# Two-layer encoder trunk: MLP passes that share their PSUM banks, and the making of the first product's forms divided anew over the engines

## The chip, the cores and the metric

The kernel runs on one core of one Trainium2 chip. A core has a matrix engine (TensorE, PE in the profile, with its weight loads as PEld), a vector engine (VectorE, DVE), a scalar engine (ScalarE, ACT), a general engine (GpSimd, POOL) and a queue of its own for transfers (SyncE, SP). Each engine works off its own list of instructions in order and waits for the others by semaphores. Products land in PSUM, which is used here as 8 banks of 128 x 512 float32; everything else lies in SBUF. The metric is the device time of one execution in microseconds (us).

## The reference

The input is 256 tokens of 2048 values. Layer 0 mixes tokens with a Conformer convolution, layer 1 with latent attention; each is followed by the MLP that this document is about. Cut to that:

```python
def sq_relu_mlp(h, w1, w2):
    return jnp.square(jax.nn.relu(h @ w1)) @ w2

for layer in range(2):                       # D_MODEL = 2048, D_FF = 8192
    x = x + mixer(rms_norm(x, norm_mixer_g[layer]))
    h = rms_norm(x, norm_mlp_g[layer])
    x = x + sq_relu_mlp(h, mlp_w1[layer], mlp_w2[layer])
```

All of it is float32, and the products are made with near float32 accuracy: each operand is split into a rounded part `hi` and a rest `lo`, and hi x hi, hi x lo and lo x hi are added (three matmuls for one product).

## The kernel before

**Chunks and the stream.** Both products of the MLP are cut into *units*, each with one transfer of 1 MB of weights (`raw`), and units into *chunks*. The chunks of a whole layer stand in one list, `chunks`, and `stream` (L423) writes the program from it. `prep` of a chunk splits its weights: ACT writes `hi` (L420), DVE writes `lo` (L421). `run` of a chunk emits its matmuls. Before the `run` of chunk n, the preparations up to chunk n + 5 are written (`WB` = 6 buffers), or up to n + 4 where the chunk is marked `tight` (`LOOK_UP` = 5). Since each engine works in order, this order is all there is of scheduling. Small jobs stand in a list `todo`; one of them is popped before each preparation (L457).

**First product (`up_units`, L485).** The 8192 columns of `w1` are cut into 4 parts `q`, each into 8 pairs `p` of two units. An up unit has two chunks of 8 x (one matmul of 512 columns and one of 256) into one PSUM bank. After its second chunk ACT copies the bank to `U` (L510). When both units of a pair are done, three jobs enter `todo`: `square` (DVE: sum of the two halves, L522, and max(0, v) x v in one instruction, L525 or L536), an empty one, and `part`, which splits the result into `hi` and `lo` by ACT and DVE. For pairs in `SEVENS`, `square` also makes seven forms of the result in a tile `W` by three subtractions on POOL (L529, L532, L533); their split parts are `sh` and `sl`. For the other pairs the parts are `gh` and `gl`. The pairs of a part are made in the order `MADE`.

**Second product (`down_units`, L547).** A *pass* is one part `q` times one half `n2` of the 2048 output columns: 8 passes per layer. 5 of its 8 pairs (3 or 2 in the last part) are multiplied by a scheme of 7 products in place of 8 (a *seven unit*, four chunks: `one`, `two`, `t13`, `t24`, for whose weights DVE makes sums in a tile `T`, L672 and L685); the other pairs are *plain units* of two chunks. The seven sums live in seven banks (P1, P2, P4, Q3, Q5, Q6, Q7); the plain products add into P2, Q3, P4 and an eighth, Q0. So while seven banks are held, one is left for an up unit. After the last seven unit `early` evicts P1, Q5, Q6, Q7 (two ACT copies, L587 and L588; four DVE additions; four DVE updates of the residual `xs`, L564). After the last plain unit `end` adds the other four banks to `xs` (L564).

**The order of chunks.** The up units of part 0 come first. Then, for each part, its two passes, `n2` = 0 and 1, are woven with the 16 up units of the next part, eight per pass: `MIX` = (2, 1, 1, 2, 1, 1, 2) says how many halves of seven units follow each up unit; three plain units close the pass, with the eighth up unit after the first of them. The last part's passes run alone.

Of the kernel before, what the change touches and what calls it, by code (L numbers as in the profile page):

```python
# [14 lines left out]
AF = mybir.ActivationFunctionType  # L15
# [67 lines left out]
def trunk_kernel(  # L83
# [339 lines left out]
    def stream(chunks, todo, pool):  # L423
# [49 lines left out]
    def mlp(layer, ssq, next_gain, finish=None, before=None, last_w1=None):  # L473
# [11 lines left out]
        def up_units(hs, q, p, extra):  # L485
# [4 lines left out]
            def up_unit(b):  # L490
                ps = []

                def chunk(h):
# [20 lines left out]
                    return Chunk(prep, run, [square, lambda: None, part] + extra if b == 1 else [], now=out)  # L514
# [4 lines left out]

            def square():  # L520
                v = held["u"][:, :, :S]
                nc.vector.tensor_tensor(v, v, held["u"][:, :, S:], op=ALU.add)  # L522
                if p in sevens:
                    f = f_tile()
                    nc.vector.scalar_tensor_tensor(  # L525
                        out=f[:, 0:4, :].rearrange("p (b t) n -> p b (t n)", b=2), in0=v, scalar=0.0, in1=v,
                        op0=ALU.max, op1=ALU.mult,
                    )
                    nc.gpsimd.tensor_tensor(  # L529
                        f[:, 4:6, :], f[:, 0:1, :].broadcast_to([P, 2, P]), f[:, 1:3, :], op=ALU.subtract  # L530
                    )
                    nc.gpsimd.tensor_tensor(f[:, 6, :], f[:, 1, :], f[:, 5, :], op=ALU.subtract)  # L532
                    nc.gpsimd.tensor_tensor(f[:, 7, :], f[:, 3, :], f[:, 6, :], op=ALU.subtract)  # L533
# [13 lines left out]
        def down_units(mp, hs, q, n2):  # L547
# [9 lines left out]
            banks, seen = {}, set()  # L557
# [16 lines left out]
            def plain(p, k, part, n, t):  # L574
                gh, gl = (a[:, k, t * P : (t + 1) * P] for a in hs[p])
                bs = n - na
                mm(outs[t, n], gh, gl, part[0][:, bs, :], part[1][:, bs, :], p == last_plain and k == 1)

            def early():
# [24 lines left out]
                return [first, second, third, fourth]  # L604

            def end():
                for t, n in ((0, nb), (1, nb), (1, na), (0, na)):
# [47 lines left out]
            def seven_unit(p):  # L655
# [4 lines left out]
                def run(names):  # L660
                    def fn(parts):
                        for name, f, key, i in names:
                            part = parts[key]
                            mm(name, *gh_gl(f), part[0][:, i, :], part[1][:, i, :],
                               p == last_seven and name in ("P1", "Q5", "Q6", "Q7"))
# [21 lines left out]
                def t24(raw, parts):  # L687
# [9 lines left out]
                        now=todo_early if p == last_seven else None,  # L697
# [3 lines left out]
            def todo_early():  # L701
                first, *others = early()
                first()
# [10 lines left out]
        with ExitStack() as cx:  # L714
# [17 lines left out]
            hs = {}  # L732
            for unit in ups(hs, 0):
                put(unit)
            for q in range(PARTS):
                now, hs = hs, {}
                more = ups(hs, q + 1) if q < PARTS - 1 else []
                for n2 in range(NNB // 2):
                    units = down_units(mp, now, q, n2)
                    if not more:  # L740
                        for unit in units:
                            put(unit)
                        continue
                    halves = [(units[p], cs) for p in SEVENS[layer][q] for cs in ((0, 1), (2, 3))]
                    for n in MIX:
                        put(more.pop(0))
                        chunks[-1][0].chunks[1].tight = n == 1
                        for unit, cs in halves[:n]:
                            put(unit, cs)
                        del halves[:n]  # L750
# [993 lines left out]
```

## Time and profile before

| | |
|---|---|
| median of 3 runs | 1973.39 us (1971.7 to 1975.42) |
| the profiled execution | 1973.36 us, of which the profile's span is 1971.2 us |
| granted TensorE clock, mean | 0.998 |
| MLP of layer 0 | about 318.6 to 970 us of the span |
| MLP of layer 1 | about 1271.9 us to the end |
| six passes woven with up units, layer 0 | 84.9, 87.4, 84.8, 87.5, 87.1, 84.5 us |

The six passes are the stretches from 409.8, 494.7, 582.1, 666.9, 754.4 and 841.5 us to 926 us; each boundary is the start of a pass's first up unit. In the profile a row gives line, engine, operation, `out<-in` tiles and shapes. Busy time of PE is not a measure of its work alone, since matmuls overlap and their ends are modelled: the distance between the starts of two matmuls says more. A time in square brackets is idle time of the engine ahead of the instruction, with what ended it.

### The profile page before, as it was taken

How to read it: one execution, taken by the hardware profiler on the slowest of the kernel's cores; microseconds unless marked ns; L12 is line 12 of the kernel's file. 1: busy time of each engine (PE TensorE's matmuls, PEld its weight loads, DVE VectorE, ACT ScalarE, POOL GpSimd, SP SyncE). 2: the span in 40 equal slices, each digit the busy share in tenths (PEclk: the TensorE clock that was granted, in tenths of full speed). 3: DMA queues.
4: the chain of work that ended last, by engine and by line, in shares of the span. 5: the costliest groups of instructions: out<-in, count | busy, mean ns of one | idle time of the engine just before them, and what ended most of it. 6: DMA issues, size and time to landing. Idle time of an engine off the chain costs nothing.

```text
span 1971.2 us, 28450 instructions
## 1 busy us (share of the span) xinstructions
PE 1937.5 (98%) x10850; PEld 1685.6 (86%) x10850; DVE 1623.1 (82%) x2241; ACT 1108.2 (56%) x1555; POOL 348.9 (18%) x289
## 2 busy tenths in 40 slices
PE   7999999999999999999999999999999999999998
PEld 7999888888888888888899998888888888888886
DVE  5999866688898898989976675567989898888987
ACT  5556655565555564555566665555645555565544
POOL 5999300210110111000001410002011002010000
PEclk9999999999999999999999999999999999999999
DMA  8666457657566666756646445665766666657663
GB/s 238 177 189 176 147 185 192 194 169 225 152 212 193 194 198 185 217 170 211 213 143 183 121 143 188 196 185 161 214 187 208 182 209 191 192 179 207 224 203 107
DMA packets 407112, 367.62 MB, mean 186 GB/s; under 512 B 15416, under 2 KB 351936, under 8 KB 406720
## 3 DMA queue, kind: packets, MB, share of 16 engines
q1 hardware_dynamic: 405952, 363.63, 61.7%
q10 hardware_dynamic: 1024, 2.17, 0.3%
q8 instruction: 85, 1.39, 0.3%
q14 instruction: 51, 0.42, 0.1%
HBM read 363.68 MB, written 2.10 MB: 186 GB/s over the span
## 4 chain that ended last, share of the span: by engine, by line
PE 85%; DVE 6%; POOL 3%; ACT 3%; issue 2%; DMA 0%; SPq 0%; POOLq 0%; DVEq 0%; ACTq 0%
PE acc L504 20%; PE acc L197 14%; PE acc L195 14%; PE acc L196 14%; PE acc L505 10%; DVE lo L421 3%; PE acc L816 3%; PE acc L815 3%; PE acc L814 3%; POOL W L529 1%; DVE T L685 1%; ACT hi L420 1%; ACT sh L420 1%; POOL W L533 1%; POOL W L532 1%
## 5 line engine op out<-in xcount | busy, mean ns | idle before, releaser
L504 PE MATMUL acc<-xt,hi 128*128 128x512 f32 x2048 | 717.4, 393 | 0.0
L421 DVE TENSOR_TENSOR lo<-raw,hi 128x1024 fp32r<-128x1024 f32 (+1 forms) x512 | 582.8, 1162 | 46.7 <-ACT hi L420 46.0
L420 ACT ACTIVATE hi<-raw 128x1024 fp32r<-128x1024 f32 (+1 forms) x512 | 495.0, 994 | 143.3 <-PE acc L196 86.6
L505 PE MATMUL acc<-xt,lo 128*128 128x256 f32 x2048 | 574.1, 280 | 0.0
L504 PEld LDWEIGHTS acc<-xt,hi 128*128 128x128 f32 x2048 | 384.4, 188 | 87.5
L505 PEld LDWEIGHTS acc<-xt,lo 128*128 128x128 f32 x2048 | 385.2, 188 | 3.7
L197 PE MATMUL acc<-lo,sh 128*128 128x512 f32 x698 | 274.2, 393 | 6.3 <-DVE lo L421 6.3
L195 PE MATMUL acc<-hi,sh 128*128 128x512 f32 x698 | 274.9, 394 | 3.1 <-ACT hi L420 3.1
L529 POOL TENSOR_TENSOR W<-W 128x256 f32<-128x256 f32 x35 | 55.6, 1588 | 1136.9 <-DVE W L525 1009.6
L420 ACT ACTIVATE hi<-T 128x1024 fp32r<-128x1024 f32 x140 | 148.1, 1058 | 152.5 <-DVE T L685 98.8
L196 PE MATMUL acc<-hi,sl 128*128 128x512 f32 x570 | 222.3, 390 | 0.0
L169 ACT ACTIVATE hi<-raw 128x1024 fp32r<-128x1024 f32 (+2 forms) x184 | 180.0, 1006 | 44.8 <-PE acc L196 41.0
L421 DVE TENSOR_TENSOR lo<-T,hi 128x1024 fp32r<-128x1024 f32 x140 | 170.9, 1221 | 29.1 <-ACT hi L420 26.5
L510 ACT ACTIVATE U<-acc 128x512 f32<-128x512 f32 x128 | 76.0, 594 | 202.6 <-PE acc L505 202.6
L170 DVE TENSOR_TENSOR lo<-raw,hi 128x1024 fp32r<-128x1024 f32 (+2 forms) x118 | 132.9, 1144 | 67.8 <-ACT hi L169 62.2
L916 DVE SCALAR_TENSOR_TENSOR sum<-ub,w_dw,sum 128x256 f32<-128x256 f32 x400 | 162.9, 485 | 7.6 <-ACT sum L872 6.5
L197 PEld LDWEIGHTS acc<-lo,sh 128*128 128x128 f32 x698 | 131.1, 188 | 40.0 <-DVE lo L421 11.5
L170 POOL TENSOR_TENSOR lo<-raw,hi 128x1024 fp32r<-128x1024 f32 x66 | 157.4, 2407 | 24.1 <-ACT hi L169 24.1
L195 PEld LDWEIGHTS acc<-hi,sh 128*128 128x128 f32 x698 | 131.0, 188 | 32.8 <-ACT hi L420 5.6
L195 PE MATMUL acc<-hi,gh 128*128 128x512 f32 x384 | 149.6, 390 | 0.0
L197 PE MATMUL acc<-lo,gh 128*128 128x512 f32 x384 | 149.5, 389 | 0.0
L196 PE MATMUL acc<-hi,gl 128*128 128x512 f32 x384 | 149.4, 389 | 0.0
(264 smaller groups left out, 3088.9 us busy)
## 6 DMA issues: line engine op xcount, KB each, us to landing
raw<-in_mlp_w SPq DMA_DIRECT2D x256, 1024.0 KB, 6.1
raw<-in_conv_w_pw SPq DMA_DIRECT2D x64, 512.0 KB, 5.5
raw<-in_conv_w_pw SPq DMA_DIRECT2D x16, 1024.0 KB, 5.1
raw<-in_mla_w_o SPq DMA_DIRECT2D x16, 1024.0 KB, 5.5
raw<-in_mla_w_kv_up SPq DMA_DIRECT2D x8, 1024.0 KB, 5.5
raw<-in_mla_w_in SPq DMA_DIRECT2D x8, 576.0 KB, 3.8
raw<-in_mla_w_in SPq DMA_DIRECT2D x4, 1024.0 KB, 6.6
raw<-in_mla_w_q_up SPq DMA_DIRECT2D x16, 256.0 KB, 3.7
```

Source lines behind the costliest of these rows:

```text
L169: nc.scalar.activation(hi, raw[:, js, :], AF.Copy)
L170: eng.tensor_tensor(lo, raw[:, js, :], hi.bitcast(F32), op=ALU.subtract)
L195: nc.tensor.matmul(ps, sh, mh, start=start, stop=False)
L196: nc.tensor.matmul(ps, sl, mh, start=False, stop=False)
L197: nc.tensor.matmul(ps, sh, ml, start=False, stop=stop)
L420: nc.scalar.activation(parts[0], src, AF.Copy)
L421: nc.vector.tensor_tensor(parts[1], src, parts[0].bitcast(F32), op=ALU.subtract)
L504: nc.tensor.matmul(ps[0], wh[:, j, :], xhl(k), start=k == 0, stop=False)
L505: nc.tensor.matmul(ps[0][:, :S], wl[:, j, :], xh(k), start=False, stop=k == KC - 1)
L510: nc.scalar.activation(held["u"][:, b, :], ps[0], AF.Copy)
L529: nc.gpsimd.tensor_tensor(f[:, 4:6, :], f[:, 0:1, :].broadcast_to([P, 2, P]), f[:, 1:3, :], op=ALU.subtract)
L916: nc.vector.scalar_tensor_tensor(out=out, in0=ubs[c][:, w : w + S], scalar=tap(c, w), in1=pcs[c], op0=ALU.mult, op1=ALU.add)
```

## The change

In words:

1. The order of the halves alternates: part 0 takes `n2` = 1 then 0, part 1 takes 0 then 1, part 2 takes 1 then 0, part 3 takes 0 then 1. Neighbouring passes of two parts with the same `n2` add into the same banks (`run` holds them): the first of the two is not `final` and runs neither `early` nor an eviction in `end`, save Q0, which is added to `xs` and given back. Each layer has 5 evictions in place of 8.
2. Because a bank is needed for Q0 in the pass that isn't `final`, no up unit stands among its plain units: the mixes are `MIX_ONE` (a pass by itself), `MIX_FIRST` and `MIX_SECOND`.
3. `square` becomes four jobs: `add` (DVE sum), an empty one, `square` (ACT: Relu, then Square), `forms` (three subtractions, now on DVE), then `part`. Two jobs are popped at once while more than four wait.
4. Pairs are made in the order 0, 3, 1, 4, 2, 5, 6, 7.
5. In `early` the two ACT copies come at once and the first two DVE additions as the next job.

```diff
-MIX = (2, 1, 1, 2, 1, 1, 2)
+MIX_ONE, MIX_FIRST, MIX_SECOND = (0, 2, 1, 1, 2, 1, 1, 2), (0, 2, 1, 1, 1, 1, 1, 1, 2), (2, 1, 1, 1, 1, 1, 1, 2)
-MADE = tuple((range(8),) * 3 + (last,) for last in ((0, 1, 2, 3, 5, 4, 6, 7), range(8)))
+MADE = tuple(((0, 3, 1, 4, 2, 5, 6, 7),) * 3 + (last,) for last in ((0, 1, 2, 3, 5, 4, 6, 7), range(8)))
...
-                if todo:
+                for _ in range(min(len(todo), 2 if len(todo) > 4 else 1)):
                     todo.pop(0)()
                 prep()
...
-                    return Chunk(prep, run, [square, lambda: None, part] + extra if b == 1 else [], now=out)
+                    return Chunk(prep, run, [add, lambda: None, square, forms, part] + extra if b == 1 else [], now=out)
...
+            def add():
+                v = held["u"][:, :, :S]
+                nc.vector.tensor_tensor(v, v, held["u"][:, :, S:], op=ALU.add)
+
             def square():
                 v = held["u"][:, :, :S]
-                nc.vector.tensor_tensor(v, v, held["u"][:, :, S:], op=ALU.add)
+                nc.scalar.activation(v, v, AF.Relu)
                 if p in sevens:
-                    f = f_tile()
-                    nc.vector.scalar_tensor_tensor(
-                        out=f[:, 0:4, :].rearrange("p (b t) n -> p b (t n)", b=2), in0=v, scalar=0.0, in1=v,
-                        op0=ALU.max, op1=ALU.mult,
-                    )
-                    nc.gpsimd.tensor_tensor(
-                        f[:, 4:6, :], f[:, 0:1, :].broadcast_to([P, 2, P]), f[:, 1:3, :], op=ALU.subtract
-                    )
-                    nc.gpsimd.tensor_tensor(f[:, 6, :], f[:, 1, :], f[:, 5, :], op=ALU.subtract)
-                    nc.gpsimd.tensor_tensor(f[:, 7, :], f[:, 3, :], f[:, 6, :], op=ALU.subtract)
+                    held["f"] = f = f_tile()
+                    nc.scalar.activation(f[:, 0:4, :].rearrange("p (b t) n -> p b (t n)", b=2), v, AF.Square)
                     held["src"], shape, tag, n = f[:, 1:8, :], [P, 7, P], "s", N_S
                 else:
-                    nc.vector.scalar_tensor_tensor(out=v, in0=v, scalar=0.0, in1=v, op0=ALU.max, op1=ALU.mult)
+                    nc.scalar.activation(v, v, AF.Square)
...
+            def forms():
+                if p in sevens:
+                    f = held["f"]
+                    nc.vector.tensor_tensor(
+                        f[:, 4:6, :], f[:, 0:1, :].broadcast_to([P, 2, P]), f[:, 1:3, :], op=ALU.subtract
+                    )
+                    nc.vector.tensor_tensor(f[:, 6, :], f[:, 1, :], f[:, 5, :], op=ALU.subtract)
+                    nc.vector.tensor_tensor(f[:, 7, :], f[:, 3, :], f[:, 6, :], op=ALU.subtract)
...
-            banks, seen = {}, set()
+            banks, seen = held
...
-                def first():
+                def copies():
                     nc.scalar.activation(s1, banks["P1"], AF.Copy)
                     nc.scalar.activation(s5, banks["Q5"], AF.Copy)
+
+                def first():
                     nc.vector.tensor_tensor(u, s1, banks["Q6"], op=ALU.subtract)
...
             def end():
+                if not final:
+                    xs_add(na, banks.pop("Q0"), 0)
+                    seen.remove("Q0")
+                    return
...
-                for n2 in range(NNB // 2):
+                for n2 in ((0, 1) if q % 2 else (1, 0)):
+                    final = q == PARTS - 1 or n2 == 1 - q % 2
+                    units = down_units(now, q, n2, run, final)
...
+                        mix = MIX_SECOND if begun else MIX_ONE if final else MIX_FIRST
+                        for i, n in enumerate(mix):
+                            if i > 0:
+                                put(more.pop(0))
+                                chunks[-1][0].chunks[1].tight = n == 1
...
+                        for i, p in enumerate(plain):
+                            if i == 1 and final:
+                                put(more.pop(0))
+                            put(units[p])
...
+                    begun = not final
+                    if final:
+                        run = ({}, set())
```

`todo_early` runs only in a `final` pass, and the marks that close a bank's sum are set only there (for Q0 in every pass).

More of the change, by code (lines that the diff above doesn't have):

```diff
@@ L576, in plain @@
                 bs = n - na
-                mm(outs[t, n], gh, gl, part[0][:, bs, :], part[1][:, bs, :], p == last_plain and k == 1)
+                mm(outs[t, n], gh, gl, part[0][:, bs, :], part[1][:, bs, :], (final or (t, n) == (0, na)) and p == last_plain and k == 1)
             def early():
@@ L602, in fourth @@
                     xs_add(na, v, 0)
-                return [first, second, third, fourth]
+                return [copies, first, second, third, fourth]
             def end():
+                if not final:
+                    xs_add(na, banks.pop("Q0"), 0)
+                    seen.remove("Q0")
+                    return
                 for t, n in ((0, nb), (1, nb), (1, na), (0, na)):
@@ L696, in seven_unit @@
                         t24, run([("Q6", S2, "t24", 0), ("P4", A22, "t24", 1)]),
-                        now=todo_early if p == last_seven else None,
+                        now=todo_early if final and p == last_seven else None,
                     ),
@@ L701, in todo_early @@
             def todo_early():
-                first, *others = early()
-                first()
+                copies, *others = early()
+                copies()
                 todo[:0] = others
@@ L730, in ups @@
                 ]
-            hs = {}
+            hs, run, begun = {}, ({}, set()), False
             for unit in ups(hs, 0):
```

26 lines of the change are left out of this document (10 added, 16 removed).

## The prediction

> **What bounds the kernel now.** I read the page's busy shares first, then the waits of TensorE (PE), then the MLP stages pass by pass, and last the order of time around one stop.
>
> ```profile
> PE 1937.5 (98%) x10850; PEld 1685.6 (86%) x10850; DVE 1623.1 (82%) x2241; ACT 1108.2 (56%) x1555; POOL 348.9 (18%) x289
> ```
>
> PE is busy for 98% of the span, and the change leaves the number of its products as it is. So a gain can only come from the moments in which PE stands still or is stretched. The table of waits shows few of them:
>
> ```profile
> ACT sh L420 <- POOL W L533: 103.0, 25, 4.7
> ...
> PE acc L197 <- DVE lo L421: 6.3, 12, 0.5
> ...
> PE acc L195 <- ACT hi L420: 3.1, 6, 0.7
> ```
>
> Columns are us in total, times, longest. PE stops 12 + 6 = 18 times, 9.4 us as idle time. All 18 lie in the MLPs: two neighbouring passes, as windows, show how unevenly (columns: length, then busy us and count for PE, PEld, DVE, ACT, POOL, then clock and DMA):
>
> ```profile
> 494.70:582.10 87.40, 85.73 (x434) 72.01 (x433) 77.15 (x80) 48.02 (x56) 14.29 (x12) 1.00 0.65 193
> 582.10:666.90 84.80, 84.80 (x434) 72.23 (x433) 76.27 (x83) 47.79 (x56) 3.70 (x3) 1.00 0.66 199
> ```
>
> Same PE work, same granted clock, 2.6 us apart. DVE has nearly the same load in both (77 and 76 us). What differs is POOL: four pairs of the next part are made into seven forms in the slow pass, one in the fast one. One stop of the slow pass, engine by engine. PE:
>
> ```profile
> 518.20 0.40 PE L195 MATMUL acc<-hi,sh 128*128 128x512 f32 x1
> ...
> 518.89 0.40 PE L195 MATMUL acc<-hi,sh 128*128 128x512 f32 x1
> ...
> 519.82 0.39 PE L196 MATMUL acc<-hi,sl 128*128 128x512 f32 x1
> 520.73 0.50 PE L197 MATMUL acc<-lo,sh 128*128 128x512 f32 x1 [0.52 <-DVE lo L421]
> 521.06 0.40 PE L195 MATMUL acc<-hi,sh 128*128 128x512 f32 x1
> ...
> 521.76 0.40 PE L504 MATMUL acc<-xt,hi 128*128 128x512 f32 x1
> ...
> 522.11 0.40 PE L504 MATMUL acc<-xt,hi 128*128 128x512 f32 x1
> ```
>
> A matmul normally starts 0.23 us after the one before (0.69 for the three of a product, 518.20 to 518.89). Here 0.91 us pass, then 0.33 (the restart costs a tenth): 0.78 lost, not the 0.52 shown. 18 such stops are 18 x 0.78 = 14.0 us. Why VectorE (DVE) is late, ScalarE (ACT), GpSimd (POOL) and DVE show:
>
> ```profile
> 510.77 0.60 ACT L510 ACTIVATE U<-acc 128x512 f32<-128x512 f32 x1 [4.72 <-PE acc L505]
> 511.26 1.05 ACT L420 ACTIVATE hi<-T 128x1024 fp32r<-128x1024 f32 x1
> 516.33 0.95 ACT L420 ACTIVATE sh<-W 128x896 fp32r<-128x896 f32 x1 [4.01 <-POOL W L533]
> 517.18 1.04 ACT L420 ACTIVATE hi<-raw 128x1024 fp32r<-128x1024 f32 x1
> 518.13 1.05 ACT L420 ACTIVATE hi<-T 128x1024 fp32r<-128x1024 f32 x1
> ...
> 520.03 0.57 ACT L510 ACTIVATE U<-acc 128x512 f32<-128x512 f32 x1
> ```
>
> ```profile
> 512.96 1.59 POOL L529 TENSOR_TENSOR W<-W 128x256 f32<-128x256 f32 x1 [22.69 <-DVE W L525]
> 514.63 0.79 POOL L532 TENSOR_TENSOR W<-W 128x128 f32<-128x128 f32 x1
> 515.50 0.79 POOL L533 TENSOR_TENSOR W<-W 128x128 f32<-128x128 f32 x1
> ```
>
> ```profile
> 511.40 0.69 DVE L522 TENSOR_TENSOR U<-U 128x512 f32<-128x512 f32 x1 [3.03 <-ACT U L510]
> 512.12 0.69 DVE L525 SCALAR_TENSOR_TENSOR W<-U 128x512 f32<-128x512 f32 x1
> 512.73 1.22 DVE L421 TENSOR_TENSOR lo<-T,hi 128x1024 fp32r<-128x1024 f32 x1
> 513.99 1.98 DVE L685 TENSOR_TENSOR T<-T,raw 128x512 f32<-128x512 f32 x2
> 517.31 1.09 DVE L421 TENSOR_TENSOR sl<-W,sh 128x896 fp32r<-128x896 f32 x1 [1.34 <-ACT sh L420]
> 518.32 1.22 DVE L421 TENSOR_TENSOR lo<-raw,hi 128x1024 fp32r<-128x1024 f32 x1
> 519.45 1.22 DVE L421 TENSOR_TENSOR lo<-T,hi 128x1024 fp32r<-128x1024 f32 x1
> ```
>
> DVE is ahead until the copy of the pair's second product (U) at 510.77; 3.03 us of waiting show it. Then the chain runs copy, sum, max and square, POOL's three subtractions (3.3 us), `sh`, `sl`; ACT sits 4.01 us behind POOL with two finished weight blocks queued behind that `sh`. The `lo<-T` that PE needs at 520.05 (519.82 + 0.23) starts at 519.45 and ends after 520.59. So the POOL chain, standing in ACT's queue, is what ends last at a stop.
>
> **The change part by part.** *Fewer evictions.* Of 8 passes per layer, 3 no longer evict the seven banks: each drops 2 ACT copies, 4 DVE additions and 7 of 8 DVE updates of `xs` (the bank of the plain products is still added). Rows:
>
> ```profile
> L564 DVE SCALAR_TENSOR_TENSOR xs<-acc,r,xs 128x512 f32<-128x512 f32 x64 | 44.0, 743 | 5.1 <-PE acc L197 5.1
> ...
> L590 DVE TENSOR_TENSOR W<-W,acc 128x512 f32<-128x512 f32 x16 | 11.0, 686 | 0.5
> ...
> L350 ACT ACTIVATE scratch<-xs 128x512 f32<-128x512 f32 x32 | 20.2, 631 | 10.2 <-DVE msp L1685 4.7 <-DVE xs L564 3.9 <-DVE xs L336 1.2
> ...
> L899 DVE TENSOR_TENSOR sum<-sum,tp 128x256 f32<-128x256 f32 x15 | 6.4, 424 | 0.2
> ...
> L1497 DVE TENSOR_SCALAR pr<-pr,zs 128x128 f32<-128x128 f32 x16 | 4.9, 305 | 0.6
> ```
>
> DVE: 6 x (4 x 0.686 + 7 x 0.743) = 47.7 us; ACT 12 x 0.6 = 7 us. None of it stops PE today (no stop follows an eviction), so alone it is worth nothing; it buys slack at the start of the next pass.
>
> *Max and square.* 64 DVE instructions of 0.69 (L525, L536) go, 44 us; 128 on ACT come, priced by its Square of the same size, 0.63: 81 us. ACT then has 1108 + 81 - 7 = 1182 us of 1971, 60%. They lie beside DVE's `lo` of the next block.
>
> *Seven forms on DVE.* 35 times three subtractions. One of 256 columns is 0.42 by L899; one of 128 columns has no subtraction row on DVE, so between nothing and 0.42; I take 0.31 from the scalar multiply of that size. 0.42 + 2 x 0.31 = 1.04 us each (0.42 to 1.27), 36 us in all. DVE altogether: -48 - 44 + 36 = -56 us. POOL loses 35 times the 3.3 us above, and it ran beside DVE:
>
> ```profile
> L685 DVE TENSOR_TENSOR T<-T,raw x140: 691/692/1117, 409.4 to 1928.1; 128x512 f32<-128x512 f32 x140
> ```
>
> An update of `T` takes 692 ns in the median (columns: least, median, most); the two at 513.99, beside POOL, took 1.98 us: 0.6 lost for one pair. The Trainium skill ("SBUF — State Buffer", section "SBUF: two separate sides") says that a GpSimd instruction and a DVE instruction with two SBUF inputs take turns on one port pair, the loser blocked for the whole instruction. The 0.6 us against POOL's 1.59 agrees in kind and is less than a whole block; by the page a whole 1.6 us of DVE per pair would come free instead of 0.6, and the sum, which counts stops alone, would be the same.
>
> *The stop, replayed by hand.* In the changed kernel's order DVE does, after a U copy of a seven-form pair: sum, `lo<-T`, two `T` updates, three subtractions, `lo<-raw`, the awaited `lo<-T`, and only then `sl`. From 511.40, with start-to-start times of the rows above: 0.72 + 1.26 + 1.38 + 1.04 + 1.13 + 1.22 = 6.75, done at 518.15. PE wants it at 520.05: 1.9 us in hand where 0.5 to 0.7 was missing. ACT meanwhile: U to 511.26, `hi` to 512.2, max and square to 513.5, the two `hi` at 514.4 and, after the `T` updates at 514.8, 515.8: never behind DVE. What is late next is `sl`, wanted only in the next pass. A whole cycle of two up units and one seven unit takes PE 4 x 2.8 + 4.83 = 16.0 us (an up chunk is 8 x 0.35 = 2.8; seven products 7 x 0.69); DVE needs 4 x 1.13 + 6.6 (the seven unit: five `lo`, three sums) + 0.72 + 1.04 + 1.01 = 13.9, plus about 1 us of waiting for ACT's max and square.
>
> *Order of pairs and banks.* Pairs of seven forms are spread (2 and 3 per pass instead of 1 and 4). One place stays tight: in part 3, the third pair of the pass with two part-sums, followed by half a seven unit, one up unit and a whole seven unit. DVE there: U copy 0.6, then 0.72 + 3 x 1.13 + 0.6 + 1.04 + 2 x 1.26 + 1.38 + 1.01 = 10.7, plus 0.5 for ACT; PE wants it after 4 x 0.69 + 5.6 + 5 x 0.69 = 11.8. 0.0 to 0.6 in hand. I allow one stop there per layer, 2 x 0.8 = 1.6 us. Over two passes seven banks stay taken and one serves the up units; that was so within a pass too (a copy 1.6 us late, 520.03, still ended before 521.76).
>
> *The sum*, against the profiled execution (1971.2 of span, 2.2 around it, 1973.4; the median of the runs is 1973.4 too): 1973.4 - 14.0 + 1.6 = 1961.0 us.
>
> **The rivals.** *Half stays.* DVE's cycle is 15 of 16 us; were forms at 1.27 and the ACT wait at 2 us, the margin would be gone in passes with three seven-form pairs, and about half of the stops would return: 1973.4 - 7 = 1966. For it: DVE at 77 of 87 us in the slow pass. Against: the fast pass runs at 76 of 85 without one stop.
>
> *ACT becomes the supplier (slower).* With one free bank, an up unit's first matmul waits for the copy of the up unit before it, and that copy now has max, square and a wait for DVE's subtractions ahead of it in ACT's queue. Three products (2.07 us) lie between, the copy takes 0.57: it decides from a start 1.5 us late. 38 up units per layer sit in passes that share banks; 0.3 us at each is 2 x 38 x 0.3 = 23 us, less the 14 of the old stops: 1982. For it: the copy at 520.03 was 1.6 late. Against: that lateness came from the 4.01 us behind POOL. The Trainium skill ("ScalarE: Activation LUTs", section "Rules for kernel authors") sends relu, max and mul to VectorE and speaks against this part; here 0.69 on DVE against 2 x 0.63 on ACT agrees, but ACT has the room.
>
> *No change.* The stops move with the order of chunks instead of going (the lead is set by 5 or 6 buffers): 1973. Against: the fast passes with the same buffers have none.
>
> **How the numbers follow.** Forecast 0.60, half 0.21, no change 0.09, slower 0.10. A difference under 0.2% (4 us) can't be told from none. Faster 0.81, same 0.09, slower 0.10. The likeliest case runs from all stops gone and 2.6 instead of 2.3 us per slow pass (1957) to 1965; with the half case and some of "no change" the range is 1956.5 to 1971.
>
> **What would show it.** Right: no ACT wait on POOL in the MLPs, PE's waits on L421 and L420 down from 9.4 to about 1 us, all passes near 84.8 us, DVE near 1570 and ACT near 1180 us. A stop left in part 3 before the last seven unit confirms the tight place. Wrong: PE waiting for ACT's U copies (slower case), or as many stops at other places.

## The result and the profile after

| | before | after |
|---|---|---|
| median of the runs | 1972.55 us (4 runs, 1971.67 to 1975.42) | 1956.55 us (4 runs, 1956.52 to 1958.31) |
| ratio of the two, 95% interval | | 0.9919 (0.9901 to 0.9936) |
| profiled execution, its span | 1973.36, 1971.2 us | 1956.55, 1954.7 us |

The kernel became faster by 0.8%, with an interval clear of no change. The forecast was 1961.0 us, range 1956.5 to 1971: the sign and the mechanism came as forecast, and the time lies at the lower edge of the range, 0.05 us inside it.

The busy shares of the kernel after:

```profile
PE 1930.4 (99%) x10850; PEld 1686.7 (86%) x10850; DVE 1554.6 (80%) x2216; ACT 1176.5 (60%) x1671; POOL 223.8 (11%) x184
```

The number of matmuls is the same. DVE has 68.5 us less than before, ACT 68.3 more, POOL 125.1 less. What PE waited for over the whole run, as the table of waits for PE alone (us in total, times, longest), and from the full table the wait of ACT for the seven forms:

```profile
PE tr L291 <- DMA stage<-in_conv_b_dw: 12.1, 1, 12.1
PE sum L883 <- DVE ub L858: 1.1, 1, 1.1
PE acc L1522 <- DVE pr L1516: 1.1, 2, 0.9
PE acc L834 <- DVE xt L208: 0.5, 1, 0.5
PE acc L1122 <- DVE cn L1112: 0.3, 1, 0.3
```

```profile
ACT sh L420 <- DVE W L544: 16.7, 12, 1.4
```

The two rows in which PE waited for `lo` (L421) and `hi` (L420), 18 times in all, are gone. What is left lies at the start and in the mixers, and none of it is in an MLP. ACT's 103.0 us of waiting behind POOL have become 16.7 behind DVE. Two stretches of 86 us in the woven passes of layer 0, as windows (columns as before), one with the most DVE work and one with little:

```profile
408.10:494.00 85.90, 85.90 (x442) 73.18 (x441) 76.63 (x95) 57.36 (x71) 0.00 (x0) 1.00 0.65 196
...
666.00:752.00 86.00, 86.00 (x436) 73.06 (x435) 71.87 (x80) 53.73 (x65) 0.00 (x0) 1.00 0.67 196
```

PE is busy for the whole length of both, where the slow pass of before was 1.67 us short of it; POOL does nothing here any more. By the starts of PE's matmuls the six woven passes of layer 0 run from 408.09 to 916.96 us: 84.8 each, as the prediction named for a sign of being right.

The place in the kernel after that answers to the one replayed by hand (second pass, end of the last pair). DVE from the sum of the pair to the awaited `lo`, and PE at the matmul that needs it:

```profile
525.56 0.69 DVE L522 TENSOR_TENSOR U<-U 128x512 f32<-128x512 f32 x1 [3.01 <-ACT U L510]
526.51 1.23 DVE L421 TENSOR_TENSOR lo<-T,hi 128x1024 fp32r<-128x1024 f32 x1 [0.26 <-ACT hi L420]
527.77 1.42 DVE L696 TENSOR_TENSOR T<-T,raw 128x512 f32<-128x512 f32 x2
529.11 0.42 DVE L540 TENSOR_TENSOR W<-W 128x256 f32<-128x256 f32 x1
529.56 0.29 DVE L543 TENSOR_TENSOR W<-W 128x128 f32<-128x128 f32 x1
529.89 0.29 DVE L544 TENSOR_TENSOR W<-W 128x128 f32<-128x128 f32 x1
530.10 1.22 DVE L421 TENSOR_TENSOR lo<-raw,hi 128x1024 fp32r<-128x1024 f32 x1
531.23 1.22 DVE L421 TENSOR_TENSOR lo<-T,hi 128x1024 fp32r<-128x1024 f32 x1
532.37 1.08 DVE L421 TENSOR_TENSOR sl<-W,sh 128x896 fp32r<-128x896 f32 x1
```

```profile
533.98 0.39 PE L196 MATMUL acc<-hi,sl 128*128 128x512 f32 x1
534.21 0.39 PE L197 MATMUL acc<-lo,sh 128*128 128x512 f32 x1
```

The engine takes 532.37 - 525.56 = 6.81 us to the end of the awaited `lo` (6.75 by hand), and PE takes that `lo` at 534.21, 0.23 us after the matmul before it: no stop, 1.84 us in hand (1.9 by hand).

*A second thing differs between the two profiles.* The 16 up units of part 0, at the start of each MLP, run alone on PE. As windows, for layer 0 and layer 1, before and then after:

```profile
318.59:409.77 91.18, 91.18 (x521) 79.29 (x520) 63.49 (x88) 48.08 (x65) 14.37 (x12) 1.00 0.64 179
1271.85:1361.35 89.50, 89.50 (x521) 78.74 (x520) 58.06 (x60) 48.05 (x62) 14.26 (x12) 1.00 0.65 183
```

```profile
318.59:408.09 89.50, 89.50 (x520) 78.75 (x520) 61.65 (x93) 55.73 (x79) 0.00 (x0) 1.00 0.66 183
1262.90:1352.40 89.50, 89.50 (x521) 78.74 (x521) 56.27 (x65) 55.59 (x76) 0.00 (x0) 1.00 0.65 183
```

The same work takes 91.18 or 89.50 us, though PE never waits and the granted clock is 1.00 in all four. In all profiles of this study such a phase has one of these two lengths, without regard to the kernel (the last section has more). To compare kernels, the table below therefore takes 1.68 us off the span for each slower phase in its profile. "PE lost" is summed from the starts of all matmuls in the MLPs: each distance over 0.3 us, less the normal 0.23. Four distances of 0.31 to 0.32 us that stand alike in every kernel, at the start of an MLP and in the last pass of layer 0, are left out. (That last pass ends at 1011 us before and at 1001 after; the 970 us in the table of the times before is too early.) A ratio is against runs of the kernel before on the same chip.

| kernel | median (lowest to highest, runs), us | ratio to before | span | slower phases | span without them | PE lost |
|---|---|---|---|---|---|---|
| before | 1972.55 (1971.67 to 1975.42, 4) | | 1971.2 | 1 | 1969.5 | 14.2 |
| after | 1956.55 (1956.52 to 1958.31, 4) | 0.9919 (0.9901 to 0.9936) | 1954.7 | 0 | 1954.7 | 0 |
| e1_forms_dve | 1961.33 (1960.31 to 1962.13, 4) | 0.9938 (0.9924 to 0.9953) | 1960.2 | 2 | 1956.8 | 1.2 |
| e2_no_sharing | 1958.32 (1956.52 to 1959.99, 4) | 0.9923 (0.9907 to 0.9940) | 1956.5 | 1 | 1954.8 | 0 |
| e3_sharing_only | 1969.28 (1967.28 to 1971.12, 10) | 0.9980 (0.9971 to 0.9990) | 1967.2 | 1 | 1965.5 | 9.7 |
| e4_pool_forms | 1958.31 (1956.40 to 1960.02, 4) | 0.9923 (0.9908 to 0.9938) | 1956.3 | 1 | 1954.6 | 0 |
| e5_square_dve | 1959.16 (1956.46 to 1960.01, 4) | 0.9921 (0.9905 to 0.9938) | 1958.2 | 2 | 1954.8 | 0 |
| e7_made_in_order | 1958.21 (1 run) | | 1956.4 | 1 | 1954.7 | 0 |
| e6_load2 | 1962.63 (1 run) | | 1960.8 | 2 | 1957.4 | 2.4 |
| e6_load4 | 1980.45 (1978.63 to 1981.85, 5) | 1.0033 (1.0020 to 1.0046) | 1978.6 | 1 | 1976.9 | 20.0 |
| e8_nosharing_load2 | 1966.38 (1 run) | | 1964.6 | 0 | 1964.6 | 9.5 |
| e8_nosharing_load4 | 1998.62 (1998.03 to 2001.04, 4) | 1.0128 (1.0113 to 1.0143) | 1996.2 | 0 | 1996.2 | 39.2 |
| e9_jobs_only | 1970.31 (1970.20 to 1972.07, 10) | 0.9992 (0.9982 to 1.0002) | 1968.2 | 0 | 1968.2 | 13.0 |
| e10_jobs_square_act | 1958.30 (1956.42 to 1960.10, 4) | 0.9928 (0.9910 to 0.9946) | 1954.3 | 0 | 1954.3 | 0 |

PE lost 14.2 us in the stops of before and loses nothing after; the spans, without the slower phase, are 1969.5 - 1954.7 = 14.8 us apart. So nearly all of the gain is the 18 stops. The other 0.6 us belong to them too, by about as much: before, the six up units that follow a stop by one product take 5.65 us and not 5.56 (521.76 to 527.41 us behind the stop that the prediction quotes, against 512.64 to 518.20 for the up unit ahead of it); the last section comes back to this. What else differs, 0.4 us in the MLPs and 0.4 in the mixer between them, has opposite signs and cancels.

### The profile page after: what moved, and what is told of

It reads as the page before. It is cut to its first block, busy times and chain, and to the rows that moved or that the text cites. A ratio compares the mean times of both kernels' runs of the same rounds, so it can differ in the third digit from the quotient of the medians.

```text
span 1954.7 us, 28298 instructions
## 1 busy us (share of the span) xinstructions
PE 1930.4 (99%) x10850; PEld 1686.7 (86%) x10850; DVE 1554.6 (80%) x2216; ACT 1176.5 (60%) x1671; POOL 223.8 (11%) x184
## 3 DMA queue, kind: packets, MB, share of 16 engines
q8 instruction: 85, 1.39, 0.3%
## 4 chain that ended last, share of the span: by engine, by line
PE 97%; DVE 1%; ACT 1%; DMA 1%; POOL 0%; issue 0%; DVEq 0%; ACTq 0%
PE acc L504 24%; PE acc L195 15%; PE acc L197 15%; PE acc L196 15%; PE acc L505 12%; PE acc L835 3%; PE acc L834 3%; PE acc L833 3%; PE acc L251 1%; PE sum L883 0%; PE acc L1531 0%; DMA xs<-in_x 0%; PE acc L1395 0%; PE acc L1396 0%; PE acc L1397 0%; PE acc L234 0%
## 5 line engine op out<-in xcount | busy, mean ns | idle before, releaser
L421 DVE TENSOR_TENSOR lo<-raw,hi 128x1024 fp32r<-128x1024 f32 (+1 forms) x512 | 576.3, 1147 | 107.0 <-ACT hi L420 106.7
L420 ACT ACTIVATE hi<-raw 128x1024 fp32r<-128x1024 f32 (+1 forms) x512 | 496.2, 994 | 135.7 <-PE acc L196 115.3
L420 ACT ACTIVATE hi<-T 128x1024 fp32r<-128x1024 f32 x140 | 148.3, 1059 | 131.7 <-DVE T L696 78.3
L421 DVE TENSOR_TENSOR lo<-T,hi 128x1024 fp32r<-128x1024 f32 x140 | 171.2, 1223 | 60.7 <-ACT hi L420 58.5
L833 PE MATMUL acc<-xt,hi 128*128 128x256 f32 x512 | 145.3, 284 | 0.0
```

What stands on the lines that cost most here:

```text
L420: nc.scalar.activation(parts[0], src, AF.Copy)
L421: nc.vector.tensor_tensor(parts[1], src, parts[0].bitcast(F32), op=ALU.subtract)
L833: nc.tensor.matmul(o, wh[:, bs], xh(k), start=k == 0, stop=False)
```

## The experiments

The change has several parts. The theory was that the stops came from POOL's chain of subtractions in ACT's queue, so that the part that takes this chain away is what pays, and the sharing of banks, the order of pairs and the move of max and square do not pay by themselves.

**The subtractions alone (e1).** The kernel before, with its three subtractions on DVE and nothing else changed:

```diff
-                    nc.gpsimd.tensor_tensor(
+                    nc.vector.tensor_tensor(
                         f[:, 4:6, :], f[:, 0:1, :].broadcast_to([P, 2, P]), f[:, 1:3, :], op=ALU.subtract
                     )
-                    nc.gpsimd.tensor_tensor(f[:, 6, :], f[:, 1, :], f[:, 5, :], op=ALU.subtract)
-                    nc.gpsimd.tensor_tensor(f[:, 7, :], f[:, 3, :], f[:, 6, :], op=ALU.subtract)
+                    nc.vector.tensor_tensor(f[:, 6, :], f[:, 1, :], f[:, 5, :], op=ALU.subtract)
+                    nc.vector.tensor_tensor(f[:, 7, :], f[:, 3, :], f[:, 6, :], op=ALU.subtract)
```

> The kernel before with one edit: the three subtractions of the seven forms on VectorE, still inside the one job `square`; passes not shared, max and square on VectorE. Theory (the 18 stops come from ScalarE's queue standing behind GpSimd's 3.3 us chain): the wait of ScalarE on GpSimd is gone, the awaited `lo<-T` is done about 0.3 us before TensorE wants it (0.72 + 0.61 + 1.04 + 1.26 + 1.38 + 1.01 + 1.13 + 1.22 = 8.37 from the start of the sum at 511.40, so 519.77 against 520.05), and at least two thirds of the stops go although VectorE gets 36 us more work: 1958 to 1964 us. Rival (VectorE's load is the limit and the GpSimd wait only its symptom): with 36 us more on VectorE the stops stay or grow: 1972 us or more.

Measured 0.9938 (0.9924 to 0.9953). All 18 stops are gone; six hitches of about 0.2 us (start to start, the restart with it) stay, 1.2 us in all. ACT at the place that the prediction quoted, in the timeline of this run:

```profile
510.70 0.60 ACT L510 ACTIVATE U<-acc 128x512 f32<-128x512 f32 x1 [4.71 <-PE acc L505]
511.19 1.05 ACT L420 ACTIVATE hi<-T 128x1024 fp32r<-128x1024 f32 x1
513.89 0.96 ACT L420 ACTIVATE sh<-W 128x896 fp32r<-128x896 f32 x1 [1.65 <-DVE W L533]
```

`sh` stands in the same place of ACT's queue and waits 1.65 us instead of 4.01; it starts 3.2 us after the copy where it was 5.6. This one edit brings 12.7 of the 14.8 us, although DVE has more to do than before (1637.0 us, 84% of the span). So a busier DVE was no danger; the wait was.

**The change without the sharing (e2).** The kernel after, with each pass evicting its own banks, the old order of halves and of pairs:

```diff
-MADE = tuple(((0, 3, 1, 4, 2, 5, 6, 7),) * 3 + (last,) for last in ((0, 1, 2, 3, 5, 4, 6, 7), range(8)))
+MADE = tuple((range(8),) * 3 + (last,) for last in ((0, 1, 2, 3, 5, 4, 6, 7), range(8)))
...
-                for n2 in ((0, 1) if q % 2 else (1, 0)):
-                    final = q == PARTS - 1 or n2 == 1 - q % 2
+                for n2 in range(NNB // 2):
+                    final = True
```

> The changed kernel without shared banks: every pass evicts for itself, with the halves in the order 0, 1, the mix and the order of pairs of the kernel before; max and square on ScalarE, forms on VectorE as a job of its own. Theory (sharing only buys slack that no stop needs): all or nearly all stops gone, 1956 to 1960 us. Rival (the 48 us of evictions that sharing takes off VectorE are what lets it keep up): stops return in the passes with four seven-form pairs, 1964 us or more.

The span without slower phases is 1954.8, that of after 1954.7: the sharing, with the new order of pairs, is worth nothing to the time here. It does take work from DVE: 1594.8 us here against 1554.6, so 40.2 us (47.7 in the prediction).

**The sharing alone (e3).** The kernel after (its order of pairs too), with the first product's jobs as they were before (max and square on DVE, subtractions on POOL, one job popped, first two additions of `early` with their copies):

```diff
-                for _ in range(min(len(todo), 2 if len(todo) > 4 else 1)):
+                if todo:
                     todo.pop(0)()
...
-                    return Chunk(prep, run, [add, lambda: None, square, forms, part] + extra if b == 1 else [], now=out)
+                    return Chunk(prep, run, [square, lambda: None, part] + extra if b == 1 else [], now=out)
...
-                return [copies, first, second, third, fourth]
+                return [first, second, third, fourth]
```

> The changed kernel with shared banks, mixes and order of pairs, but the first product as in the kernel before: max and square in one VectorE instruction and the seven forms on GpSimd, in the three jobs. Theory: the 4 us wait of ScalarE behind GpSimd stays at every pair of seven forms; where such a pair is followed by the first half of a seven unit, TensorE still stops: about 5 places per layer at 0.78 us, 1956.6 + 8 = 1964 us (1960 to 1970). Rival (sharing is the gain): no stops, 1957 us.

Measured 0.9980 (0.9971 to 0.9990), 4.0 us less span than before. Its waits:

```profile
ACT sh L420 <- POOL W L533: 96.7, 25, 4.0
...
PE acc L197 <- DVE lo L421: 5.7, 11, 0.5
```

ACT waits behind POOL 25 times as before. 13 stops are left of 18, at other places. Sharing and spreading together take away five of the stops, not their cause; which of the two does it was not tried.

**Which engine, once the jobs are apart (e4, e5), and the order of pairs (e7).** e4 is the kernel after with its three subtractions on POOL again, in the new job `forms`. e5 is the kernel after with max and square in one DVE instruction, in the new job `square`. e7 is the kernel after with the pairs made in the order 0 to 7. Their cores:

```diff
-                    nc.vector.tensor_tensor(
+                    nc.gpsimd.tensor_tensor(
                         f[:, 4:6, :], f[:, 0:1, :].broadcast_to([P, 2, P]), f[:, 1:3, :], op=ALU.subtract
                     )
```

> The changed kernel with only the three subtractions back on GpSimd, in the place of the new job `forms`. By the order of ScalarE's queue, max and square end at 513.5 in the replayed example, GpSimd at 516.8, and ScalarE comes to `sh` at 515.8, behind the two weight blocks that it held up before: 1 us of waiting, nothing urgent behind it. Theory that the place in the queue matters: 0 to 4 stops, 1956.5 to 1960 us. Rival (it matters that GpSimd does it: its 3.3 us and its slowing of VectorE): half of the stops return, 1963 us or more.

```diff
-                nc.scalar.activation(v, v, AF.Relu)
...
-                    nc.scalar.activation(v, v, AF.Square)
+                    nc.vector.scalar_tensor_tensor(out=v, in0=v, scalar=0.0, in1=v, op0=ALU.max, op1=ALU.mult)
```

> The changed kernel with max and square back in one VectorE instruction (0.69 us, 64 times, 44 us), in the place of ScalarE's two; the rest as changed. Theory (the forms on VectorE and the order of the jobs settle it, the split of max and square over engines does not): no stops, the time of the changed kernel within its steps, 1956.5 to 1960 us. Rival (ScalarE's part is needed since VectorE is at its limit): stops in the passes with three seven-form pairs, 1962 us or more.

```diff
-MADE = tuple(((0, 3, 1, 4, 2, 5, 6, 7),) * 3 + (last,) for last in ((0, 1, 2, 3, 5, 4, 6, 7), range(8)))
+MADE = tuple((range(8),) * 3 + (last,) for last in ((0, 1, 2, 3, 5, 4, 6, 7), range(8)))
```

> The changed kernel with the pairs of parts 0 to 2 made in the order 0 to 7, so that one pass makes one seven-form pair and the next four, as in the kernel before. Theory (spreading the pairs is not needed once ScalarE does not wait on GpSimd): no stops, 1956.5 to 1960 us. Rival (spreading is needed): stops of about 0.8 us in three passes per layer, 1961 us or more.

All three have no stop and the span of after to within 0.1 us. None of these parts is needed by itself. In e4 POOL's chain is there again, and ACT waits for it 21.9 us in 13 waits instead of 103.0 in 25: what matters is less who subtracts than when the chain has to be done. e4 also tells what POOL costs DVE: DVE is busy 1542.8 us, while after without its subtractions (35 x 1.0) would be 1519.6. Most of the 23 us between are DVE instructions stretched beside POOL: those of e4 that overlap one of its subtractions take 19.6 us more in all than the median of their kind, 0.56 us per pair.

**How much slack there is (e6), and what the sharing adds to it (e8).** The kernel after with two or four DVE instructions more behind the subtractions of each seven-form pair, on a half of `U` that nothing reads any more (e6), and the same without the sharing, as in e2 (e8). With four:

```diff
+                    for _ in range(4):
+                        nc.vector.tensor_tensor(
+                            held["u"][:, :, S:], held["u"][:, :, S:], held["u"][:, :, S:], op=ALU.max
+                        )
```

> The changed kernel with four additional VectorE instructions of 0.69 us on dead data behind the forms of each seven-form pair (35 pairs, 97 us in all): a measure of the slack that is left. By the replay 1.9 us are in hand at the place of the old stop and 2.76 are added, and the cycle rises from about 15 to 17.7 us against TensorE's 16. Theory: TensorE stops again, about 1 us at most seven-form pairs outside the first pass, 1966 to 1985 us. Rival (VectorE's order, not its load, decides; the lead of five to six chunks takes up the load): 1957 to 1960 us.

At the replayed place, DVE and PE in the timeline of the run with four:

```profile
531.83 2.87 DVE L546 TENSOR_TENSOR U<-U 128x512 f32<-128x512 f32 x4
...
535.71 0.39 PE L196 MATMUL acc<-hi,sl 128*128 128x512 f32 x1
...
535.75 1.22 DVE L421 TENSOR_TENSOR lo<-T,hi 128x1024 fp32r<-128x1024 f32 x1
...
536.88 1.08 DVE L421 TENSOR_TENSOR sl<-W,sh 128x896 fp32r<-128x896 f32 x1
537.02 0.50 PE L197 MATMUL acc<-lo,sh 128*128 128x512 f32 x1 [0.92 <-DVE lo L421]
```

Four more instructions move `lo` back by 4 x 0.69 = 2.76 us. With 1.84 in hand it should come 0.92 too late. It is done at 536.88, where PE was due for it at 535.71 + 0.23 = 535.94: 0.94 too late. (PE starts 0.14 after that, 1.08 late from start to start. The 0.92 in brackets is another quantity, the time since the modelled end of the matmul before, and equals the forecast by chance.) The hand replay of DVE's queue is a true picture of the place.

> The changed kernel with two instead of four additional VectorE instructions of 0.69 us per seven-form pair (48 us). Four of them cost 22 us. Theory: the 1.9 us in hand at the old place take up 1.38 of them, the cycle reaches 16.3 us against 16.0: 0 to 4 stops, 1954.7 to 1958 us of span and up to 3.4 more where the up phases run at their slower cadence. Rival (the cost is in proportion to the load): half of 22, 1965 us.

With two, PE stops at exactly two places, one in each layer: while part 3 is made, inside the last seven unit of the pass with two part-sums, at its sixth product. It is the "tight place" of the prediction, whose sum counts five products of that unit first. PE there in layer 0:

```profile
810.89 0.39 PE L196 MATMUL acc<-hi,sl 128*128 128x512 f32 x1
812.21 0.50 PE L197 MATMUL acc<-lo,sh 128*128 128x512 f32 x1 [0.94 <-DVE lo L421]
```

In the kernel after, the same `lo` and the matmul that takes it:

```profile
807.84 1.22 DVE L421 TENSOR_TENSOR lo<-T,hi 128x1024 fp32r<-128x1024 f32 x1
...
809.34 0.39 PE L197 MATMUL acc<-lo,sh 128*128 128x512 f32 x1
```

DVE starts on the next block at 808.97, when it is done with this one, and PE takes it at 809.34: 0.37 us are in hand, inside the 0.0 to 0.6 of the prediction. With about 1.3 us added, PE is 810.89 + 0.23 = 811.12 to 812.21, 1.09 us, late.

> The changed kernel without shared banks (as in e2_no_sharing) with the same four additional VectorE instructions per seven-form pair. Theory (sharing buys VectorE slack, 48 us of it, that no stop needs as long as the load is low): here it is slower than the same load with sharing by 10 to 40 us. Rival (sharing is worth nothing even then): within 3 us of it.

> The changed kernel without shared banks with two additional VectorE instructions per seven-form pair. Theory (without sharing the slack is smaller by some 48 us over 16 passes, 3 us each, and four seven-form pairs stand in one pass): stops return, 1962 to 1975 us. Rival (sharing matters only near the four-instruction load): 1958 us.

Without the sharing the same load costs 1964.6 - 1957.4 = 7.2 us more with two (six long stops instead of two) and 1996.2 - 1976.9 = 19.3 us more with four. So the sharing does buy slack on DVE, as the prediction said; this kernel has no use for it. By an estimate, about 5 of the 19.3 us come through PE's clock, which falls to half after some of the longer stops (last section).

**Is the order of the jobs enough (e9, e10)?** e4 suggested that the place of the chain in the queues decides, and not the engines. e9 is the kernel before with the four jobs and the popping of after, but every operation on its old engine and no sharing:

```diff
+                for _ in range(min(len(todo), 2 if len(todo) > 4 else 1)):
...
+                    return Chunk(prep, run, [add, lambda: None, square, forms, part] + extra if b == 1 else [], now=out)
...
             def square():
                 v = held["u"][:, :, :S]
                 if p in sevens:
                     held["f"] = f = f_tile()
                     nc.vector.scalar_tensor_tensor(
...
+            def forms():
+                if p in sevens:
+                    f = held["f"]
+                    nc.gpsimd.tensor_tensor(
```

> The kernel before with the job of the first product cut into four (sum, empty, max and square, forms) and popped as in the changed kernel, but every operation on its old engine: max and square on VectorE, forms on GpSimd; no shared banks, old order of pairs. By the replay GpSimd's chain then ends near 518.7, ScalarE comes to `sh` at 515.8 and waits 2.9 us, with no block behind it that TensorE needs before `sh` is through, and the awaited `lo<-T` ends at 518.15 - 1.04 + 0.61 = 517.7 against 520.05. Theory (what has to go is `sh` from its place ahead of two weight blocks; engines and banks don't matter): 0 to 6 stops, 1956.5 to 1961 us. Rival (GpSimd has to be left out, or the banks shared, as well): 12 stops or more, 1966 us or more.

Here the theory fell: 0.9992 (0.9982 to 1.0002). PE loses 13.0 us in place of 14.2. The waits of this run, and in its timeline the place of the prediction's stop on ACT, POOL and PE:

```profile
ACT sh L420 <- POOL W L546: 79.6, 25, 4.8
...
PE acc L504 <- ACT U L510: 4.0, 6, 0.7
...
PE acc L197 <- DVE lo L421: 3.1, 4, 0.8
```

```profile
509.51 1.05 ACT L420 ACTIVATE hi<-T 128x1024 fp32r<-128x1024 f32 x1
...
514.02 1.59 POOL L542 TENSOR_TENSOR W<-W 128x256 f32<-128x256 f32 x1 [25.27 <-DVE W L528]
...
517.59 0.95 ACT L420 ACTIVATE sh<-W 128x896 fp32r<-128x896 f32 x1 [3.14 <-POOL W L546]
...
518.97 0.39 PE L197 MATMUL acc<-lo,sh 128*128 128x512 f32 x1
...
519.40 0.58 ACT L510 ACTIVATE U<-acc 128x512 f32<-128x512 f32 x1
...
520.03 0.50 PE L504 MATMUL acc<-xt,hi 128*128 128x512 f32 x1 [0.67 <-ACT U L510]
```

The job that makes max and square on DVE now stands later in DVE's queue. Counted from the `hi<-T` that follows the pair's copy, POOL starts after 514.02 - 509.51 = 4.51 us; in the kernel before it was 512.96 - 511.26 = 1.70. `sh` stands later in ACT's queue too, but not late enough: ACT still waits 3.14 us behind POOL. Now the next U copy (519.40) comes too late, and PE waits for the bank: the mechanism of the "slower" rival, at work in a kernel that is not the changed one. Six of the stops are of this kind; at four PE still waits for `lo`, as the waits show.

e10 is the kernel after with its subtractions on POOL and without the sharing (the edits of e4 and e2 together). From e9 it differs by max and square on ACT, and by the earlier copies in `early` (point 5 of the change).

> As e9_jobs_only (no shared banks, old order of pairs, forms on GpSimd in their own job), but with max and square on ScalarE. In e9 GpSimd started at 514.02, since VectorE made max and square only behind the updates of `T`, and ScalarE's wait of 3.14 us at `sh` pushed the next U copy to 519.40, so that TensorE waited for a bank. With max and square on ScalarE they end 2.9 us after the U copy begins (511.9), GpSimd ends near 515.2, ScalarE comes to `sh` at 514.2 and waits 1 us, and the next U copy is on time at 516.7. Theory (what decides is when GpSimd's chain may start and what stands behind it; neither shared banks nor the new order of pairs is needed): 0 to 4 stops, 1956.4 to 1962 us. Rival (with GpSimd in the chain the shared banks or the spread pairs are needed): 8 stops or more, 1964 us or more.

No stop; the span is 1954.3, that of after 1954.7. ACT, POOL and DVE in its timeline, at the same place:

```profile
509.49 1.05 ACT L420 ACTIVATE hi<-T 128x1024 fp32r<-128x1024 f32 x1
...
511.81 0.74 POOL L540 TENSOR_TENSOR W<-W 128x256 f32<-128x256 f32 x1 [23.67 <-DVE lo L421]
...
511.84 2.13 DVE L696 TENSOR_TENSOR T<-T,raw 128x512 f32<-128x512 f32 x2
...
515.03 0.93 ACT L420 ACTIVATE sh<-W 128x896 fp32r<-128x896 f32 x1
...
516.82 0.57 ACT L510 ACTIVATE U<-acc 128x512 f32<-128x512 f32 x1
```

With the square on ACT, POOL starts 511.81 - 509.49 = 2.32 us after that `hi`, `sh` finds its forms ready, and the copy follows in time. DVE's two updates of `T` are again stretched beside POOL (2.13 us instead of 1.42), and it does no harm. Between e9 and e10 lie 1968.2 - 1954.3 = 13.9 us. Point 5 was not tried apart from this, but none of the stops quoted here is at an eviction, and the lateness that made them is gone with the earlier square.

None of the variants is faster than the kernel after: those without stops that ran more than once end on the same floor (lowest runs 1956.40 to 1956.52 us), with PE's matmuls one behind the other throughout the MLPs.

## Why the prediction was right

*The bound* was named rightly: PE's stops, and behind them ACT standing behind POOL's three subtractions. e1 shortens just this wait (from 4.01 to 1.65 us at the place quoted) and the 18 stops go. The forecast case (all stops gone) came, and the rivals did not: not half of the stops stay (none does), PE never waits for a U copy in the kernel after, and no new stops come at other places.

*The costs by part.* A whole set of subtractions takes 0.42 + 0.29 + 0.29 = 1.00 us (0.42 + 2 x 0.31 = 1.04 predicted). Relu and Square take 0.62 and 0.64 (0.63). ACT has 1176.5 us (1182). DVE lost 68.5 us instead of 56: the sum left out that DVE instructions are no longer stretched beside POOL. The prediction showed this effect (0.6 for one pair) and e4 measured it (about 20 us for all), but it was not taken into DVE's total. The two savings on DVE are nearer 40.2 (sharing, e2) and 36.6 (max and square: 1591.2 in e5 less 1554.6) than 47.7 and 44: the prediction counted whole durations, and in the profile an instruction of DVE often starts up to a tenth of a us before the one ahead of it ends. Not one of these differences touched the time. The Trainium skill ("SBUF — State Buffer", section "SBUF: two separate sides") has the loser of the shared port blocked for the whole of the other's instruction, and the rows agree with that more closely than the prediction said. It set its 0.6 against the whole 1.59 of POOL's first subtraction; but that ran to 512.96 + 1.59 = 514.55, the update of `T` came at 513.99, and what was left, 0.56 us, is what the two updates lost (1.98 less 1.42). In e10 they lose 2.13 - 1.42 = 0.71, beside a subtraction of 0.74 that began just ahead of them. Over all pairs of e4 the loss is 0.56 us per pair, a fifth of POOL's 2.86 (100.2 us by 35).

*Evictions.* "None of it stops PE today, so alone it is worth nothing" was right for the changed kernel (e2) and wrong for the sharing beside the old jobs: e3, with the pairs spread as well, gained 4.0 us, five stops of 18. How the slack gets from a place without stops to one with them was not traced.

*The rule against max and square on ACT.* The Trainium skill ("ScalarE: Activation LUTs", section "Rules for kernel authors") speaks for VectorE. By the instruction it is right (0.69 on DVE against 0.62 + 0.64 on ACT). In the queues it is indifferent (e5), or the other way about (e9 against e10, 13.9 us, point 5 included).

*The sum* gave 1961.0, the profile 1956.55. The 4.45 us between are: 1.6 for the allowance of one stop per layer at the tight place, the step of the prediction that failed. Its margin (0.0 to 0.6) was right, with 0.37 measured, but the sum took the worse end. 1.68 for the slower up phase that the profile of before happened to have, which a sum against a single profile carries along unseen. 0.8 because the gain without it is 14.8 and not 14.0 us; of this 0.2 is that the stops lost 14.2 us, and 0.6 the slower up units behind six of them. The remaining 0.35 is the time around the span (1.85 us instead of 2.2). The lower end of the range was made of all stops gone at 2.6 us per slow pass, without the allowance. That the time lies inside by 0.05 us is luck as far as the size goes: the same kernel also ran in 1956.52 and in 1958.31 us, and the slower phase alone moved the forecast by 1.68.

## What to carry to other kernels

When the busiest engine stops only now and then, look at the in-order queue of the engine that feeds its feeder: a wait of 4 us for a slow third engine costs nothing by itself, and starves the bound engine through the finished work queued behind it. Here a faster step (e1) cured it, and so did an earlier start of the chain with a later place in the queue (e10); the later place without the earlier start did not (e9). Once the bound engine no longer stops, slack bought elsewhere is worth nothing, so price each part of a change against the stops that are left. To know how much slack a place has, replay the queue by hand and then add a known load: the delay that appears, from start to start and taken from the load, is the slack to within 0.2 us here.

## What the runs showed of the hardware that was not expected

*Two cadences at the same clock.* The up phase alone on PE alternates matmuls of 512 and 256 columns. From one start of the 512-column form to the 32nd one after it, at the same place in layer 0, before (slower phase) and after:

```profile
349.70 0.40 PE L504 MATMUL acc<-xt,hi 128*128 128x512 f32 x1
...
361.01 0.40 PE L504 MATMUL acc<-xt,hi 128*128 128x512 f32 x1
```

```profile
349.85 0.39 PE L504 MATMUL acc<-xt,hi 128*128 128x512 f32 x1
...
360.94 0.39 PE L504 MATMUL acc<-xt,hi 128*128 128x512 f32 x1
```

A pair takes 0.353 us before (11.31 by 32), 0.347 after (11.09 by 32); 256 pairs make the 1.68 us of a phase. The rate stays the same through a whole phase, 12 of the 28 phases in the 14 profiles have the slower one, and one and the same kernel shows both in its two layers. The run times fit: 1971.6, 1973.4 and 1975.3 for the kernel before, 1956.5 and 1958.3 for the kernel after, in steps of 1.8 to 1.9 us. The slower rate also comes behind stops: before, the six up units that follow a stop by one product run at 0.353 (the 5.65 us above, by 16), and the next seven unit is at its old rate again. In none of the 14 profiles does an up unit that starts within four matmuls of a stop of over 0.4 us, from start to start, run at the faster rate. So a stop can bring the slower rate on. What brings it on for a whole phase, where PE doesn't wait, was not tried and stays open. For small differences it means comparing the lowest runs, or the spans less 1.68 us for each slower phase, and not medians of a few runs.

*A clock that halves behind stops of 1.4 us.* In e8 with four more instructions, layer 0, PE stands 1.40 us up to 560.21 and 1.39 more up to 562.34. PE from there, and then the granted clock (third number from the end) in a window:

```profile
562.34 0.80 PE L197 MATMUL acc<-lo,sh 128*128 128x512 f32 x1 [1.39 <-DVE lo L421]
562.93 0.63 PE L195 MATMUL acc<-hi,sh 128*128 128x512 f32 x1
563.36 0.63 PE L196 MATMUL acc<-hi,sl 128*128 128x512 f32 x1
```

```profile
561.40:568.10 6.70, 5.76 (x14) 4.52 (x15) 6.67 (x8) 4.95 (x7) 0.00 (x0) 0.50 0.76 245
```

Here the matmuls start 0.43 us apart instead of 0.23, for 6.8 us. The same comes twice more in layer 1, for 3.4 us each, and once for 3.4 us with the sharing (behind waits of 0.71 and 1.39 us); in the other twelve profiles it does not come between the first MLP's start and the last one's end. By an estimate from these lengths the half clock costs 13.6 / 2 = 6.8 us without the sharing and 1.7 with it, the 5 us named under e8. Not every such pair of stops does it: the same two waits end at 738.72 and 740.85 us of this run, and the clock stays at 1.00.

*A stop costs more than its wait.* The stops of before are shown as 0.52 us of idle time on average (9.4 us by 18) and cost 0.79 from start to start (14.2 by 18), since idle time counts only from the modelled end of the matmul before, and the slower restart (0.33 instead of 0.23 to the next start) is not in it.
